# The 16x16 diagonal blocks of the delta rule's triangular inverse: from TensorE to VectorE

## The chip, the core and the metric

The kernel runs on one core of a Trainium2 chip. The metric is the time of one execution in microseconds (us) on the device; lower is better. TensorE (PE in the profile, with PEld for its weight loads) multiplies matrices, VectorE (DVE) and ScalarE (ACT) work elementwise, GpSimd (POOL) does a little, and SyncE (SP) issues DMAs. ScalarE can issue DMAs too, and then spends its own time on each issue. Every engine works through its own list of instructions in order; semaphores hold an instruction back until what it reads is there.

## The reference

Two blocks follow each other: the first with stick-breaking attention, retention and two MLPs, the second with a hybrid mixer and a layer of 16384 experts. There are 256 tokens and a width of 1024. The change touches only the mixer's gated delta rule, which with its 8 heads, after a convolution, reads in short:

```python
G = jnp.cumsum(g, axis=-1)
gamma = jnp.where(incl, jnp.exp(jnp.where(incl, diff, 0.0)), 0.0)      # diff = G_c - G_s
k_beta = k * beta[..., None]
a_mat = jnp.where(strict, jnp.einsum('bnhcd,bnhsd->bnhcs', k_beta, k) * gamma, 0.0) + jnp.eye(CHUNK)
rhs = jnp.concatenate([v * beta[..., None], k_beta * jnp.exp(G)[..., None]], axis=-1)
sol = lax.linalg.triangular_solve(a_mat, rhs, left_side=True, lower=True, unit_diagonal=True)
u, w = sol[..., :DV], sol[..., DV:]
def step(S, inp):                                                       # along the chunks
    v_new = u_c - jnp.einsum('bhcd,bhde->bhce', w_c, S)
    o = jnp.einsum('bhcd,bhde->bhce', qd, S) + jnp.einsum('bhcs,bhse->bhce', at, v_new)
    S = S * dec[..., None, None] + jnp.einsum('bhcd,bhce->bhde', kt, v_new)
```

The matrix `a_mat` is triangular with ones on its diagonal. The kernel inverts it instead of solving with it, in chunks of 128 tokens, and treats the 16 meta tokens that stand ahead of the sequence as a chunk of their own.

## The kernel before

All large matmuls have both factors split into a high and a low part, so a projection is three matmuls for each 128 rows of the contraction (`mm3`, lines 88, 89 and 91). The weights stream through class `Weights`: SyncE loads a `raw` part of 128x1024 (line 247), ScalarE rounds it to `whi` (line 277), VectorE forms the rest, `wlo` (line 278). Four raw and three split parts are in flight. The normalised input, split the same way, comes from `normed`, just ahead of `small_gates`.

`Hybrid.mixers` works the mixer in two halves, q = 0 and 1, each with two units u = 2q and 2q + 1; a unit is two heads, thus four 128x128 blocks (two heads by two chunks). In a half, `main` is the row of projections (names in it: `pq`, `pv`, `pz` for the delta rule, `pqb`, `pvb` for the forgetting attention, `pg` for the gates). Beside it run several generators: the two delta units in lockstep, `meta_state`, the forgetting attention and, in the first half, another stream. `drive` takes a step of each in turn at every `yield`, and a scheduler places what they issue on the engines. So the number of `yield`s decides how many projection matmuls stand between two steps of the delta rule.

`delta_unit` builds `b`, the strictly triangular part of four blocks (tile `bu`, from the product `pkk`), and calls `inverse`, which returns `m`. Later it uses `m` for `pw` and `pvn`. `meta_state` does the same for the meta tokens: one 64x64 matrix that holds four heads' 16x16 blocks (`bm`); its `m` goes into `pvm`, from which the start state `pS0` follows, which both units need. `inverse` doubles the block size at each level l: it transposes `m` (`pt`), multiplies by `b` (`py`, masked to `y`) and by `m` again (`pm`), and subtracts:

```python
nc.vector.scalar_tensor_tensor(m, b, -1.0, mask(0), op0=OP.mult, op1=OP.mult)
...
for l in range(1, levels):
    if l >= 5:
        yield from self.merge(n, e, b, m, t, y, 1 << l)
        continue
    pt = each("pt", lambda o, i: nc.tensor.transpose(o, m[:, i, :], idn))
```

Ahead of the loop `m` is right for blocks of 2. Levels 1, 2 and 3 bring it to 16, level 4 to 32, and `merge` at levels 5 and 6 to 128. The meta matrix has `levels=4` and needs 1 to 3 alone, since its blocks are of 16.

Of the kernel before, what the change touches and what calls it, by code (L numbers as in the profile page):

```python
# [548 lines left out]
class Hybrid:  # L549
# [95 lines left out]
    def small_gates(self):  # L645
# [44 lines left out]
        z = self.ap.tile([128, 2, W], F32, name="cout")  # L690
        nc.vector.memset(z, 0.0)
        self.rows = self.hp.tile([128, W], F32R, name="rows")
        nc.vector.tensor_copy(self.rows, z[:, 0, :])
# [133 lines left out]

    def inverse(self, n, e, b, levels, w):


        k, nc = self.k, self.k.nc
        idn = k.ident[0:e, 0:e]
        shape = [e, n, e]

        def mask(l):
            return self.cmask[0:e, l:l + 1, 0:e].to_broadcast(shape)

        def each(name, f):
            p = self.bank(name)[0:e, 0:n, 0:e]
            for i in range(n):  # L840
                f(p[:, i, :], i)
            return p

        m = w.tile(shape, F32, name=f"m{n}")
        nc.vector.scalar_tensor_tensor(m, b, -1.0, mask(0), op0=OP.mult, op1=OP.mult)
        nc.vector.tensor_tensor(m, m, idn[:, None, :].to_broadcast(shape), op=OP.add)
        yield
        t = w.tile(shape, F32, name=f"t{n}")
        y = w.tile(shape, F32, name=f"y{n}")
        for l in range(1, levels):  # L850
            if l >= 5:
                yield from self.merge(n, e, b, m, t, y, 1 << l)
                continue
            pt = each("pt", lambda o, i: nc.tensor.transpose(o, m[:, i, :], idn))
            nc.scalar.activation(t, pt, AF.Copy)
            yield
            py = each("py", lambda o, i: nc.tensor.matmul(o, b[:, i, :], t[:, i, :], start=True, stop=True))
            nc.vector.tensor_tensor(y, py, mask(l), op=OP.mult)
            yield
            pm = each("pm", lambda o, i: nc.tensor.matmul(o, y[:, i, :], m[:, i, :], start=True, stop=True))  # L860
            nc.vector.tensor_tensor(m, m, pm, op=OP.subtract)
            yield
        return m
# [26 lines left out]

    def meta_state(self, q):

# [5 lines left out]
        nc.tensor.transpose(pt[0:64, 0, :], km, k.ident)  # L898
        nc.tensor.transpose(pt[0:64, 1, :], vm, k.ident)
        sq = w.tile([64, 128], F32, name="msq")  # L900
# [4 lines left out]
        nc.scalar.activation(kt, pt[0:64, 0, :], AF.Copy, scale=ss)  # L905
        v = w.tile([64, 128], F32, name="mv")
        nc.scalar.activation(v, pt[0:64, 1, :], AF.Copy)
        yield
# [30 lines left out]
        nc.vector.scalar_tensor_tensor(b[:, 0, :], pk, col[:, 0:1], gt, op0=OP.mult, op1=OP.mult)  # L939
        m = yield from self.inverse(1, 64, b, 4, w)  # L940
        pv = self.bank("pvm")[0:64, 0, :]
# [14 lines left out]
    def delta_unit(self, u, w):  # L956
# [37 lines left out]
        yield  # L994
        m = yield from self.inverse(4, 128, b, 7, w)
        while u not in self.unit:
# [155 lines left out]
    def mixers(self):  # L1152
        k, nc, a = self.k, self.k.nc, self.k.a
        xn = (klist(k.nh), klist(k.nl))
        with ExitStack() as ctx:
# [14 lines left out]
            self.tile("vm", [128, 8, M])  # L1170

            cum = self.tile("cum", [128, 128 + W])
            nc.vector.memset(cum, 1.0)
# [93 lines left out]
            def meta(q, u):  # L1267
                while u not in rows_v:
                    yield
                yield from self.meta_state(q)  # L1270

# [11 lines left out]
            for q in range(2):  # L1283
# [3 lines left out]
                             main_vb(v), main_z(v), main_qb(v), *([main_gates(3, 6)] if q else []))  # L1287
                drive(main, (delta(q), 1 + q), meta(q, v), forget((1, 2, 3) if q else (0,)),
                      *([] if q else [self.stream()]))
# [530 lines left out]
```

## Time and profile before

| | us |
|---|---|
| median of three runs | 1937.61 |
| fastest and slowest of them | 1937.57, 1942.92 |
| the profiled execution | 1950.35 |
| its span, first to last instruction | 1948.6 |

The profile is of one execution. Its clock of TensorE, as granted, is 0.997 of full speed on average. By engine, TensorE is busy for 99% of the span, VectorE for 73%, ScalarE for 57% and GpSimd for 6%. The mixer lies between about 700 and 1040 us, its halves between 700 and 1020. Weights come in all through the kernel, 332.28 MB are read and 18.87 MB are written.

In rows of instructions, `x4` is a count of instructions taken together; an arrow leads from what is read to what is written (out<-in); the sizes are partitions by elements. `<-DVE wlo L278` behind an idle time says which instruction ended it.

### The profile page before, as it was taken

What the parts mean: (1) busy time and instruction counts of PE and PEld (TensorE: products, weight loads), DVE (VectorE), ACT (ScalarE), POOL (GpSimd) and SP (SyncE); (2) the same over time, 40 slices, a digit from 0 to 9 for tenths busy, and PEclk for the clock granted to TensorE, in tenths of its full rate; (3) what the DMA queues carried; (4) which work ended last, traced back from release to release, by engine and by line L of the source; (5) the groups of instructions that cost most, each with busy time, mean ns of one, the idle gap of its engine ahead of it and who ended that gap; (6) DMA issues with size and microseconds to landing.
All of it is one profiled execution on the core that took longest, in us unless ns stands there. A gap on an engine that the chain in (4) does not pass through costs nothing.

```text
span 1948.6 us, 38035 instructions
## 1 busy us (share of the span) xinstructions
PE 1925.9 (99%) x14787; PEld 1827.2 (94%) x14787; DVE 1427.0 (73%) x2840; ACT 1119.7 (57%) x1761; POOL 116.8 (6%) x187
## 2 busy tenths in 40 slices
PE   8999999999999999999999999999999999999999
PEld 7999999999999989999899999999999998888887
DVE  6575556777655588778676699999888867777776
ACT  7776544655665465545455565446666655555554
POOL 2110000000000100110100111110000000000000
PEclk9999999999999999999899999999999999999999
DMA  6456665555666543222256446776555567777775
GB/s 196 141 164 187 190 186 195 160 179 180 204 186 191 187 158 109 95 90 87 77 173 214 138 163 220 230 227 201 179 177 176 179 198 241 241 240 238 240 239 184
DMA packets 109413, 353.63 MB, mean 181 GB/s; under 512 B 12832, under 2 KB 15664, under 8 KB 109104
## 3 DMA queue, kind: packets, MB, share of 16 engines
q1 hardware_dynamic: 97104, 329.82, 53.8%
q10 hardware_dynamic: 12128, 21.38, 3.4%
q8 instruction: 116, 1.90, 0.4%
q14 instruction: 65, 0.53, 0.1%
HBM read 332.28 MB, written 18.87 MB: 180 GB/s over the span
## 4 chain that ended last, share of the span: by engine, by line
PE 91%; DVE 5%; issue 3%; ACT 1%; DMA 0%; POOL 0%; SPq 0%; DVEq 0%; POOLq 0%; ACTq 0%
PE acc L1597 6%; PE acc L1599 6%; PE acc L1596 6%; PE ph L91 6%; PE ph L88 5%; PE ph L89 5%; PE pd L88 3%; PE pd L91 3%; PE pd L89 3%; PE pu L89 3%; PE pu L91 3%; PE pu L88 3%; PE pg L1565 3%; DVE wlo L278 2%; PE pq L88 2%
## 5 line engine op out<-in xcount | busy, mean ns | idle before, releaser
L278 DVE TENSOR_TENSOR wlo<-raw,whi 128x512 fp32r<-128x512 f32 (+1 forms) x863 | 774.3, 901 | 340.4 <-ACT whi L277 295.2
L277 ACT ACTIVATE whi<-raw 128x512 fp32r<-128x512 f32 (+1 forms) x863 | 674.0, 788 | 603.4 <-PE acc L1597 73.0
L88 PE MATMUL ph<-nh,whi 128*128 128x256 f32 x1024 | 256.1, 285 | 0.4 <-ACT whi L277 0.4
L89 PE MATMUL ph<-nl,whi 128*128 128x256 f32 x1024 | 250.6, 280 | 0.0
L1597 PE MATMUL acc<-whi,cl 128*128 128x512 f32 x504 | 198.1, 393 | 0.0
L1596 PE MATMUL acc<-whi,ch 128*128 128x512 f32 x504 | 196.7, 390 | 0.0
L88 PEld LDWEIGHTS ph<-nh,whi 128*128 128x128 f32 x1024 | 193.3, 189 | 0.6 <-ACT whi L277 0.6
L89 PEld LDWEIGHTS ph<-nl,whi 128*128 128x128 f32 x1024 | 193.4, 189 | 0.0
L91 PE MATMUL ph<-nh,wlo 128*128 128x256 f32 x1024 | 163.2, 282 | 2.1 <-DVE wlo L278 2.0
L1599 PE MATMUL acc<-wlo,ch 128*128 128x512 f32 x504 | 156.2, 391 | 0.0
L91 PEld LDWEIGHTS ph<-nh,wlo 128*128 128x128 f32 x1024 | 138.3, 189 | 3.9 <-DVE wlo L278 3.5
L88 PE MATMUL pu<-nh,whi 128*128 128x256 f32 x512 | 126.7, 282 | 0.0
L89 PE MATMUL pu<-nl,whi 128*128 128x256 f32 x512 | 126.6, 281 | 0.1
L88 PE MATMUL pd<-uh,whi 128*128 128x256 f32 x512 | 123.6, 281 | 0.0
L89 PE MATMUL pd<-ul,whi 128*128 128x256 f32 x512 | 123.5, 281 | 0.0
L1596 PEld LDWEIGHTS acc<-whi,ch 128*128 128x128 f32 x504 | 94.6, 188 | 21.6
L1597 PEld LDWEIGHTS acc<-whi,cl 128*128 128x128 f32 x504 | 94.7, 188 | 20.4
L1599 PEld LDWEIGHTS acc<-wlo,ch 128*128 128x128 f32 x504 | 94.7, 188 | 20.0
L89 PEld LDWEIGHTS pu<-nl,whi 128*128 128x128 f32 x512 | 97.1, 190 | 0.4 <-DVE nl L183 0.3
L89 PEld LDWEIGHTS pd<-ul,whi 128*128 128x128 f32 x512 | 96.9, 189 | 0.0
L88 PEld LDWEIGHTS pu<-nh,whi 128*128 128x128 f32 x512 | 96.7, 189 | 0.1
L88 PEld LDWEIGHTS pd<-uh,whi 128*128 128x128 f32 x512 | 96.7, 189 | 0.0
(553 smaller groups left out, 4226.7 us busy)
## 6 DMA issues: line engine op xcount, KB each, us to landing
raw<-expert_u SPq DMA_DIRECT2D x128, 512.0 KB, 3.8
raw<-expert_v SPq DMA_DIRECT2D x128, 512.0 KB, 4.3
raw<-w_hyb SPq DMA_DIRECT2D x72, 512.0 KB, 3.5
raw<-w_mlp_up SPq DMA_DIRECT2D x64, 512.0 KB, 4.3
raw<-w_mlp_down SPq DMA_DIRECT2D x64, 512.0 KB, 3.6
raw<-w_ret_in SPq DMA_DIRECT2D x48, 512.0 KB, 3.7
spill<-act SPq DMA_DIRECT2D x62, 256.0 KB, 2.8
act<-spill ACTq DMA_DIRECT2D x62, 256.0 KB, 3.7
```

The source lines that it names most:

```text
L88: mm(out, wh[k], xh[k], start=first and k == 0, stop=False, skip_group_check=True)
L89: mm(out, wh[k], xl[k], start=False, stop=False, skip_group_check=True)
L91: mm(out, wl[k], xh[k], start=False, stop=last and k == n - 1, skip_group_check=True)
L277: nc.scalar.activation(hi, src, AF.Copy)
L278: self.last = nc.vector.tensor_tensor(lo, src, hi.bitcast(F32), op=OP.subtract).ins
L1565: nc.tensor.matmul(pg[:, i, :], A[:, i, :], B[:, i, :], start=True, stop=True)
L1596: mm(acc[t][d], c0[i][t], vh, start=False, stop=False, skip_group_check=True)
L1597: mm(acc[t][d], c1[i][t], vh, start=False, stop=False, skip_group_check=True)
L1599: mm(acc[t][d], c0[i][t], vl, start=False, stop=False, skip_group_check=True)
```

## The change

Levels 1 to 3 leave `inverse`; its loop begins at 4. In their place the 16x16 diagonal blocks of a half, 32 for each unit and 4 for the meta matrix, are laid one on each of 68 partitions and inverted there by VectorE. To get there, ScalarE writes `b` to a DRAM tile `bd` (`to_solve`, one DMA for each of three matrices), and SyncE loads the diagonal blocks of it into `bs` (nine DMAs). `solve` works from the last row of the inverse upward: 15 times a product over the rows below (`bt`) and a sum of it into one row of `bx`. ScalarE then writes the blocks with nine DMAs into DRAM tiles `zd` and `zm` that hold zeros elsewhere; six DMAs in `small_gates` write these zeros, each from a zero tile. SyncE loads `zd` and `zm` as `m`. `bx` and `bs` are one buffer each for both halves. `meta_state` now begins when the keys' rows are there (`rows_k`), no longer the values', and takes up its values behind the writing of `b`. Both kinds of matrix wait in the program's text until `solve` has issued its writes (`self.solved`).

```diff
--- before.py
+++ after.py
@@ -689,6 +689,10 @@
 
         z = self.ap.tile([128, 2, W], F32, name="cout")
         nc.vector.memset(z, 0.0)
+        for t in self.zd:
+            nc.scalar.dma_start(t, z.rearrange("p a t -> p (a t)")[:, 0:512].rearrange("p (i t) -> p i t", i=4))
+        for t in self.zm:
+            nc.scalar.dma_start(t, z[0:64, 0:1, 0:64])
         self.rows = self.hp.tile([128, W], F32R, name="rows")
         nc.vector.tensor_copy(self.rows, z[:, 0, :])
         k.split(self.rows[0:8], self.rows[32:40], pc)
@@ -825,7 +829,51 @@
         nc.scalar.activation(eb, pg, AF.Exp)
         return pg, gt, eb
 
-    def inverse(self, n, e, b, levels, w):
+    def blocks(self, t, e, n):
+
+        return bass.AP(t.tensor, t.offset, [[e, n], [16 * n * e + 16, e // 16], [n * e, 16], [1, 16]])
+
+    def to_solve(self, q, part, b, e, n):
+
+        nc = self.k.nc
+        yield
+        t = self.dram.tile([e, n, e], F32, name=f"bd{q}{part}")
+        nc.scalar.dma_start(t, b)
+        x = self.bs[q][part:part + n * e // 16]
+        for i in range(n):
+            nc.sync.dma_start(x[i * e // 16:(i + 1) * e // 16], self.blocks(t, e, n)[i])
+        self.given[q] += 1
+        yield
+
+    def solve(self, q):
+
+
+        nc = self.k.nc
+        while self.given[q] < 3:
+            yield
+        for _ in range(3):
+            yield
+        b = self.bs[q]
+        x = self.hp.tile([68, 16, 16], F32, name="bx")
+        tmp = self.hp.tile([68, 225], F32, name="bt")
+        nc.vector.tensor_copy(x, self.eye)
+        for s in range(14, -1, -1):
+            n = 15 - s
+            t = tmp[:, 0:n * n].rearrange("p (c t) -> p c t", c=n)
+            nc.vector.scalar_tensor_tensor(t, x[:, s + 1:16, s + 1:16].rearrange("p t c -> p c t"), -1.0,
+                                           b[:, s:s + 1, s + 1:16].to_broadcast([68, n, n]), op0=OP.mult, op1=OP.mult)
+            nc.vector.tensor_reduce(x[:, s, s + 1:16], t, axis=AX.X, op=OP.add)
+            if s in (9, 4):
+                yield
+        yield
+        for part, e, n, t in ((0, 128, 4, self.zd[2 * q]), (32, 128, 4, self.zd[2 * q + 1]), (64, 64, 1, self.zm[q])):
+            for i in range(n):
+                nc.scalar.dma_start(self.blocks(t, e, n)[i], x[part + i * e // 16:part + (i + 1) * e // 16])
+        self.solved.add(q)
+        yield
+
+    def inverse(self, n, e, b, z, levels, w):
+
 
 
         k, nc = self.k, self.k.nc
@@ -842,12 +890,14 @@
             return p
 
         m = w.tile(shape, F32, name=f"m{n}")
-        nc.vector.scalar_tensor_tensor(m, b, -1.0, mask(0), op0=OP.mult, op1=OP.mult)
-        nc.vector.tensor_tensor(m, m, idn[:, None, :].to_broadcast(shape), op=OP.add)
-        yield
+        nc.sync.dma_start(m, z)
+        for _ in range(3):
+            yield
+        if levels < 5:
+            return m
         t = w.tile(shape, F32, name=f"t{n}")
         y = w.tile(shape, F32, name=f"y{n}")
-        for l in range(1, levels):
+        for l in range(4, levels):
             if l >= 5:
                 yield from self.merge(n, e, b, m, t, y, 1 << l)
                 continue
@@ -888,7 +938,7 @@
             nc.scalar.activation(m[p, :, q], pm[p, 0:n, q], AF.Copy)
         yield
 
-    def meta_state(self, q):
+    def meta_state(self, q, values):
 
         k, nc, w = self.k, self.k.nc, self.mp
         km, vm = (x[:, 4 * q:4 * q + 4, :] for x in (self.km, self.vm))
@@ -896,15 +946,12 @@
         cum, bones = self.cmask[0:64, 8, 0:64], self.cmask[0:64, 9, 0:64]
         pt = self.bank("ptk")
         nc.tensor.transpose(pt[0:64, 0, :], km, k.ident)
-        nc.tensor.transpose(pt[0:64, 1, :], vm, k.ident)
         sq = w.tile([64, 128], F32, name="msq")
         ss = w.tile([64, 1], F32, name="mss")
         nc.scalar.activation(sq, pt[0:64, 0, :], AF.Square, accum_out=ss)
         self.rsqrt(ss, ss, 1.0)
         kt = w.tile([64, 128], F32, name="mkt")
         nc.scalar.activation(kt, pt[0:64, 0, :], AF.Copy, scale=ss)
-        v = w.tile([64, 128], F32, name="mv")
-        nc.scalar.activation(v, pt[0:64, 1, :], AF.Copy)
         yield
         pb = self.bank("pbk")
         nc.tensor.transpose(pb[:, 0, 0:64], kt, k.ident[0:64, 0:64])
@@ -937,7 +984,17 @@
         nc.tensor.matmul(pk, kf, kf, start=True, stop=True)
         b = w.tile([64, 1, 64], F32, name="bm")
         nc.vector.scalar_tensor_tensor(b[:, 0, :], pk, col[:, 0:1], gt, op0=OP.mult, op1=OP.mult)
-        m = yield from self.inverse(1, 64, b, 4, w)
+        yield from self.to_solve(q, 64, b, 64, 1)
+        while not values():
+            yield
+        pt = self.bank("ptv")
+        nc.tensor.transpose(pt[0:64, 0, :], vm, k.ident)
+        v = w.tile([64, 128], F32, name="mv")
+        nc.scalar.activation(v, pt[0:64, 0, :], AF.Copy)
+        yield
+        while q not in self.solved:
+            yield
+        m = yield from self.inverse(1, 64, b, self.zm[q], 4, w)
         pv = self.bank("pvm")[0:64, 0, :]
         nc.tensor.matmul(pv, m[:, 0, :], v, start=True, stop=True)
         vn = w.tile([64, 128], F32, name="vnm")
@@ -992,7 +1049,10 @@
         nc.gpsimd.affine_select(gt, gt, pattern=[[0, 4], [1, 128]], compare_op=OP.is_ge, fill=0.0, base=0,
                                 channel_multiplier=-1)
         yield
-        m = yield from self.inverse(4, 128, b, 7, w)
+        yield from self.to_solve(u // 2, 32 * (u % 2), b, 128, 4)
+        while u // 2 not in self.solved:
+            yield
+        m = yield from self.inverse(4, 128, b, self.zd[u], 7, w)
         while u not in self.unit:
             yield
         v, qf, rq = self.unit[u]
@@ -1169,6 +1229,16 @@
             self.tile("km", [128, 8, M])
             self.tile("vm", [128, 8, M])
 
+
+            self.dram = pool("solve", 1, space=bass.MemoryType.DRAM)
+            self.bs = [self.hp.tile([68, 16, 16], F32, name="bs")] * 2
+            self.given, self.solved = [0, 0], set()
+            self.zd = [self.dram.tile([128, 4, 128], F32, name=f"zd{u}") for u in range(4)]
+            self.zm = [self.dram.tile([64, 1, 64], F32, name=f"zm{q}") for q in range(2)]
+            self.tile("eye", [68, 16, 16])
+            nc.vector.memset(self.eye, 1.0)
+            nc.gpsimd.affine_select(self.eye, self.eye, pattern=[[1, 16], [-1, 16]], compare_op=OP.is_equal, fill=0.0,
+                                    base=0, channel_multiplier=0)
             cum = self.tile("cum", [128, 128 + W])
             nc.vector.memset(cum, 1.0)
             nc.vector.tensor_copy(cum[:, 0:128], self.cmask[:, 7, :])
@@ -1265,9 +1335,9 @@
                     forgotten.add(u)
 
             def meta(q, u):
-                while u not in rows_v:
+                while u not in self.rows_k:
                     yield
-                yield from self.meta_state(q)
+                yield from self.meta_state(q, lambda: u in rows_v)
 
             def chain(*gens):
                 for g in gens:
@@ -1285,7 +1355,7 @@
                 main = chain(main_k(u), main_k(v), main_kb(u), main_v(u), main_kb(v), main_v(v),
                              self.key_norms(q, self.fb), main_vb(u), main_q(u), main_qb(u), main_q(v), main_z(u),
                              main_vb(v), main_z(v), main_qb(v), *([main_gates(3, 6)] if q else []))
-                drive(main, (delta(q), 1 + q), meta(q, v), forget((1, 2, 3) if q else (0,)),
+                drive(main, (delta(q), 1 + q), meta(q, v), self.solve(q), forget((1, 2, 3) if q else (0,)),
                       *([] if q else [self.stream()]))
 
     def gate(self, gt, p, r=None):
```

Lines behind the first hunk carry higher numbers in the changed kernel: `pt`, `py` and `pm` at 854, 857 and 860 become 904, 907 and 910.

The first place is SyncE's queue in the first half of the mixer. `raw` are the weights (`w_hyb` the mixer's, `peer_wq` the expert layer's), `gspill` a store of gate values, `bd_...` the three DRAM copies of `b`, `zd_8124` and `zd_8125` the solved blocks of the first half's two units:

```order
-L247 DMA raw<-w_hyb 128x1024 x53
-L247 DMA raw<-peer_wq 128x1024 x3
+L1324 DMA gspill<-cout 256x1x256
+L247 DMA raw<-w_hyb 128x1024 x9
+L844 DMA bs<-bd_8881 8x16x16 x4
+L247 DMA raw<-w_hyb 128x1024 x4
+L844 DMA bs<-bd_8979 8x16x16 x2
+L844 DMA bs<-bd_8937 4x16x16
+L844 DMA bs<-bd_8979 8x16x16 x2
+L247 DMA raw<-w_hyb 128x1024 x8
+L893 DMA m_9159<-zd_8124 128x512
+L893 DMA m_9166<-zd_8125 128x512
```

Before, only weights stand here. Now nine loads of diagonal blocks (4, 2, 1 and 2) lie between them, and behind eight further weights the loads of `m`, which wait for the writes of the solved blocks; that of the meta matrix and 17 weight loads stand behind the two shown.

The second place is TensorE's row where a delta unit's inverse begins. Before, this is the first level of unit 0, right behind its `pkk`; `pv` is the projection of the values, `ptv` a transpose of them:

```order
L986 MATMUL pkk<-kf 128x128 x4
L854 MATMUL pt<-ident,m_8742 128x128 x4
L91 MATMUL pv<-nh,wlo 128x272 x3
L807 MATMUL ptv<-ident,cout 128x128 x4
L91 MATMUL pv<-nh,wlo 128x272
L88 MATMUL pv<-nh,whi 128x272
L89 MATMUL pv<-nl,whi 128x272
L88 MATMUL pv<-nh,whi 128x272
L857 MATMUL py<-t_8821,bu 128x128 x4
```

In the changed kernel the first instructions that read an `m` stand further down, among the projection `pvb`: `pvm` reads the meta matrix's, `pt` those of units 0 and 1:

```order
L999 MATMUL pvm<-mv,m_9161 64x128
L88 MATMUL pvb<-nh,whi 128x272
L89 MATMUL pvb<-nl,whi 128x272
L88 MATMUL pvb<-nh,whi 128x272
L89 MATMUL pvb<-nl,whi 128x272
L1008 MATMUL pS_9259<-vnm,kth 128x128 x4
L1302 MATMUL ptv<-ident,cout 128x128 x4
L1306 MATMUL ptvm<-ident,cout 16x128 x2
L904 MATMUL pt<-ident,m_9159 128x128 x4
L904 MATMUL pt<-ident,m_9166 128x128 x4
L777 MATMUL ptq<-ident,qf 128x128 x4
L907 MATMUL py<-t_9309,bu 128x128 x4
```

The level that was first is gone; the one that is now first is level 4, the meta matrix's `pvm` comes ahead of it, and the two units' transposes stand side by side, with few matmuls between `pvm` and them.

The third place is VectorE's list at the start of the first half's `solve` (`bt` the products, `bx` the rows of the inverse). `cin` belongs to the norm of the keys, `rows` to the forgetting attention:

```order
L863 SCALAR_TENSOR_TENSOR bt<-bx,bs 68x1
L770 SCALAR_TENSOR_TENSOR cin<-cin 4x272
L865 TENSOR_REDUCE bx<-bt 68x1
L768 TENSOR_TENSOR cin<-cin 4x272
L863 SCALAR_TENSOR_TENSOR bt<-bx,bs 68x4
L769 SCALAR_TENSOR_TENSOR cin<-cin 4x272
L865 TENSOR_REDUCE bx<-bt 68x2
L770 SCALAR_TENSOR_TENSOR cin<-cin 4x272
L863 SCALAR_TENSOR_TENSOR bt<-bx,bs 68x9
L278 TENSOR_TENSOR wlo<-raw,whi 128x1024
L865 TENSOR_REDUCE bx<-bt 68x3
L1141 TENSOR_TENSOR rows<-cin 4x272
```

The solve's instructions have others between them, weight splits `wlo` among them.

## Rows read from the trace of the kernel before

**Rows 1.** The page, its first part:

```profile
span 1948.6 us, 38035 instructions
...
PE 1925.9 (99%) x14787; PEld 1827.2 (94%) x14787; DVE 1427.0 (73%) x2840; ACT 1119.7 (57%) x1761; POOL 116.8 (6%) x187
```

**Rows 2.** Windows: us, busy (count) of PE, PEld, DVE, ACT, POOL; TensorE clock; DMA:

```profile
700.00:740.00 40.00, 39.60 (x300) 36.00 (x299) 37.54 (x99) 27.66 (x53) 1.54 (x7) 1.00 0.47 153
...
sum 320.00, PE 317.23 PEld 293.03 DVE 252.73 ACT 173.07 POOL 25.22; mean PE 39.65 PEld 36.63 DVE 31.59 ACT 21.63 POOL 3.15
```

**Rows 3.** The list of TensorE's waits, 700 to 1040: total us, times, longest:

```profile
PE pto L1058 <- DVE on L1054: 0.8, 2, 0.6
```

**Rows 4.** Timeline of TensorE, 752.4 to 755.5: start, us, instruction:

```profile
752.45 0.66 PE L854 MATMUL pt<-ident,m 128*128 128x128 f32 x4
752.95 1.06 PE L860 MATMUL pm<-m,y 128*128 128x128 f32 x8
753.76 0.37 PE L91 MATMUL pv<-nh,wlo 128*128 128x272 f32 x1
754.08 1.16 PE L857 MATMUL py<-t,bu 128*128 128x128 f32 x8
755.00 0.50 PE L91 MATMUL pv<-nh,wlo 128*128 128x272 f32 x2
```

**Rows 5.** Timeline of TensorE, 939.0 to 939.3:

```profile
939.02 0.33 PE L860 MATMUL pm<-m,y 64*64 64x64 f32 x2
939.27 0.39 PE L88 MATMUL pq<-nh,whi 128*128 128x260 f32 x1
```

**Rows 6.** Groups of VectorE, 700 to 1000: busy us, mean ns, idle before:

```profile
L858 DVE TENSOR_TENSOR y<-py,cmask 128x512 f32<-128x512 f32 x16 | 11.0, 688 | 4.3 <-PE py L857 4.3
```

**Rows 7.** Timeline of VectorE, 755.9 to 758:

```profile
755.89 1.22 DVE L278 TENSOR_TENSOR wlo<-raw,whi 128x1024 fp32r<-128x1024 f32 x1
757.02 0.50 DVE L742 SCALAR_TENSOR_TENSOR cout<-cin,conv,cout 128x272 f32<-128x272 f32 x1
757.43 0.15 DVE L917 TENSOR_TENSOR bgs<-pst,hsel 64x8 f32<-64x8 f32 x1
757.55 0.50 DVE L742 SCALAR_TENSOR_TENSOR cout<-cin,conv,cout 128x272 f32<-128x272 f32 x1
```

**Rows 8.** The instruction of line 672: ns, start:

```profile
L672 ACTq DMA_DIRECT2D al<-a_log x1: 334/334/334, 684.0 to 684.0; - x1
```

**Rows 9.** DMA issues: count, KB each, us from issue to landing:

```profile
spill<-act SPq DMA_DIRECT2D x62, 256.0 KB, 2.8
act<-spill ACTq DMA_DIRECT2D x62, 256.0 KB, 3.7
...
cmask<-cmask ACTq DMA_DIRECT2D x1, 640.0 KB, 6.2
...
vec<-vec ACTq DMA_DIRECT2D x1, 1.5 KB, 2.5
...
al<-a_log ACTq DMA_DIRECT2D x1, 4.0 KB, 3.2
```

**Rows 10.** Timeline of TensorE, 953.5 to 957.5:

```profile
953.58 0.28 PE L88 MATMUL pqb<-nh,whi 128*128 128x256 f32 x1
...
955.00 0.28 PE L88 MATMUL pqb<-nh,whi 128*128 128x256 f32 x1
```

**Rows 11.** Timeline of TensorE, 926 to 928.5:

```profile
926.64 0.29 PE L88 MATMUL pvb<-nh,whi 128*128 128x272 f32 x1
...
928.14 0.28 PE L88 MATMUL pvb<-nh,whi 128*128 128x272 f32 x1
```

**Rows 12.** Window of 941 to 951, columns as in rows 2:

```profile
941.00:951.00 10.00, 10.00 (x52) 8.85 (x51) 3.60 (x7) 4.37 (x10) 2.60 (x2) 0.51 0.16 50
```

**Rows 13.** Timeline of TensorE, 947.2 to 947.5:

```profile
947.20 0.42 PE L88 MATMUL pq<-nh,whi 128*128 128x260 f32 x1
947.41 0.42 PE L89 MATMUL pq<-nl,whi 128*128 128x260 f32 x1
```

## The prediction

> **What bounds the kernel now.** I began with the page's first two parts: TensorE is busy for 1925.9 of 1948.6 us [rows 1]. Busy is not yet bound, so I went on to the windows of the stretch in which the change lies, the two halves of the hybrid mixer, 700 to 1020 us: TensorE 317.23 of 320 us, VectorE 252.73, ScalarE 173.07, and in the first 40 us VectorE is at 37.54 [rows 2]. The list of TensorE's waits decides it: the longest total from 700 to 1040 us is 0.8 us [rows 3]. TensorE stands in one program order, and every instruction finds its data there when its turn comes. So a matmul taken out is worth its step (the time to the next start), and a wait put into that row is paid in full.
>
> **What goes from TensorE.** In `inverse`, levels 1 to 3 of a delta unit go, each with four transposes `pt`, four products `py` and four `pm`; a float32 product shows as two records. The steps of one such level in a dense place: the transposes 0.50 us (752.45 to 752.95), `pm` 0.81, `py` 0.92 [rows 4], 2.23 us together. Four units by three levels: 26.8 us. A meta block's level is one transpose and two products of 64x64; `pm` takes 0.25 us (939.02 to 939.27) [rows 5], `py` has the same size, for the transpose I take 0.15: 0.65 us, six times, 3.9 us. In all 30.7 us. With the smaller step for both products and 0.4 for the transposes it is 27, with the larger for both 32. Nothing lies beside these matmuls on TensorE, so this is gained wherever the engine has other work in its row; the projections are that work.
>
> **VectorE and ScalarE.** VectorE loses eight instructions of 128x512 for each unit at about 0.69 us (`y` on line 858 [rows 6], `m` on 861 of the same size, and the two that made the first `m`): 22 us. It gains two solves. Of their sizes the trace has none; the nearest rows are a step of 0.41 us for 272 elements and 0.12 us for 8 [rows 7], so 0.11 us and 1.1 ns an element. A solve has 15 products and 15 sums over 1, 4, ... 225 elements, 1240 for each kind: 30 x 0.11 + 2480 x 0.0011 = 6.0 us; with dependent pairs back to back somewhat more, I take 6.5, at most 8. The sum for VectorE is a relief of 9 us, which is worth nothing by itself. ScalarE loses twelve copies and gains 30 DMA starts of 0.33 us [rows 8], 10 us; about even, and it has room.
>
> **What the change adds: four DMAs in a chain.** For each pair of units now stands, before level 4: blocks to DRAM (ScalarE), blocks back to 68 partitions (SyncE), solve (VectorE), nine writes of the solved blocks (ScalarE), three loads of `m` (SyncE). I count it from the meta block's product `pkk`, since the solve needs all three block sets and that one is last.
>
> First half, from that `pkk`: VectorE has four `bu`, three small ones and two 272-element ones before it ends `bm`, +3.2 us. A short DMA: 128 runs of 32 bytes landed 3.2 us after issue (`al`), 128 runs of 12 bytes in 2.5 (`vec`) [rows 9]; I take 3.2, so DRAM has the block at +6.5. SyncE then issues it and two more at 0.33 us each, the last lands at +10.7. VectorE itself comes to the solve at +10.0, so it waits under 1 us. Between the solve's instructions the order puts five weight splits `wlo` (step 1.13 us [rows 7]), fourteen instructions of some 270 elements and a few more: 12.8 us. With 6.5 the solve ends at +30. The nine writes take 9 x 0.33 us to start, and the eighth has to wait until the second has landed, since they share a completion lane: the last starts 3.9 us later and lands 3.2 after that. Then the loads: `m` of 256 KB like `act<-spill`, 3.7 us [rows 9]. All are there 10.7 us after the solve, at +40.7.
>
> TensorE's row from `pkk` to the first instruction that needs an `m` (`pvm`, line 999): 44 matmuls of a `pvb`, 48 of `pq`, 48 of `pqb`, 48 of `pq`, 48 of `pz`, 28 of `pvb`, and some 18 short ones. Twelve matmuls of 256 columns take 1.42 us [rows 10], twelve of 272 take 1.50 [rows 11]: 5.5 + 5.8 + 5.7 + 5.8 + 5.7 + 3.5 + 2.3 = 34.3 us. So TensorE comes at +34.3, finds nothing until +40.7 and stands 6.4 us.
>
> Second half, the same way: `bm` at +1.2, the blocks back at +8.2 (one DMA behind it, not three), 20 us of solve with six `wlo` between, +28.2; here TensorE needs only the first unit's `m` at once: four writes and a load, 4.5 + 3.9 = 8.4, +36.6. TensorE's row up to `pt` (line 904): 41 + 48 + 48 + 48 + 48 matmuls and short ones, 30.1 us. It stands 6.5 us.
>
> Together 12.9 us. If every DMA lands like `vec`, each chain is 3.3 us shorter and 6 us remain; if each needs the 6.2 us of `cmask` [rows 9], each is 11.5 us longer, 36 us. I take 12.9, because `al`, `spill` and `act` lie at 2.8 to 3.7 and are nearest in size.
>
> Before I took that value I weighed a rule that speaks against it. In the trace, short runs cost a read nothing: `al` with runs of 32 bytes lands in 3.2 us, 256 KB of `spill` in 2.8 [rows 9]. The Trainium skill (DMA: Bandwidth & Descriptors, Specifications) says that below 512 bytes a DMA engine does a read-modify-write; the eighteen write-backs go out in runs of 64 bytes. No row here shows a short write to DRAM, so the rule is neither borne out nor refuted; what slow transfers would do is the third rival below.
>
> **The rest.** The zeros: six DMA starts on ScalarE among the splits of the normalised input (`normed`), for which TensorE waits at that place: 6 x 0.33 us = 2.0 us if none is hidden, 0 if all; I take 1.0. What is queued behind the waits: on SyncE the weight loads behind `m` stand until the write-backs land, 7 us; six loads are ahead of TensorE (four raw, three split; one is used in 2.9 us), some 17 us, so that is covered. On ScalarE the weight split behind the nine writes comes 4.5 us late and TensorE stops for it, but inside the 6.4 us already counted. VectorE's copy of `eye` for the second half waits for the same write-backs, about 1 us, with nothing urgent behind it. After both halves the gates' projections still stand behind the delta rule's last matmul, so a late unit isn't exposed at the end. Moving the transpose of `vm` is free.
>
> **Sum.** -30.7 + 12.9 + 1.0 = -16.8 us in the profiled execution, 1950.35 us (span 1948.6 and 1.75 around it): 1933.5. The three timed runs have a median of 1937.61, 0.65% less; scaled, the gain is 16.7 and the time 1920.9 us.
>
> **Rivals.**
> 1. The chain is covered. For it: the order was laid out so that TensorE has filler, and every other wait in this stretch fits to within 0.8 us [rows 3]. Against: four landings in a row, each of which my rows put at 2.5 us or more. Gain 30.7 - 1 = 29.7, 1908 us.
> 2. The stops cost clock. The trace has one stretch, 941 to 951 us, with a granted clock of 0.51, the lower level (1.2 of 2.4 GHz) [rows 12]; small products of 64x64 as in [rows 5] stand just before it, and matmuls of 260 columns start 0.21 us apart there [rows 13], where those of 256 and 272 otherwise take 0.12 [rows 10, 11]. Such a fall costs 10 us x 0.49 = 4.9 us. If both stops bring one, the gain is 16.8 - 9.8 = 7.0, 1930.7 us. For it: these stops are longer than any TensorE has now. Against: the one fall seen had no idle time before it, and might itself go. The Trainium skill (TensorE: Matmul & The Clock Gate, HAM oscillation) describes just this, a wait for a DMA after which the next matmuls run cold; no stop of that length is in this trace to test it.
> 3. The other side, slower: the write-backs and block loads are slow, because hundreds of 64-byte runs go to and from DRAM between weight loads. Place: `pvm` and `pt`. At 6.2 us a landing the stops are 36 us, +6 in all, with two falls of the clock +16, 1953 us. It decides from about 5.4 us a landing, where the stops eat the 29.7. For it: `cmask` at 6.2 and no row of a short write. Against: the four other kinds (`spill`, `act`, `vec`, `al`), 2.5 to 3.7 [rows 9].
> 4. Between them, landings near 5 us: no change, 1932 to 1943 us.
>
> **Chances.** Forecast 0.50, rival 1 0.17, rival 2 0.13, rival 4 0.10, rival 3 0.10. The forecast's own range is 1912 to 1930 (landings of 2.5 to 4.2 us, one fall more or none). The range for 8 in 10 goes from 1906, just under rival 1, to 1938, which takes in rival 2 and half of rival 4. What can be told from no change is 0.3%, 5.8 us; rival 2 lies near that bound, and I give 0.04 of it to no change: faster 0.76, the same 0.14, slower 0.10.
>
> **What would show it.** Right: 24 products `py` of 128x128 fewer in each half; two stops of TensorE, at `pvm` in the first half and at `pt` in the second, of about 6 us, released by a DMA; solves of 6 to 8 us busy; short DMAs landing in 2.5 to 3.7 us; the mixer some 17 us shorter and nothing else changed. Wrong: stops under 2 us or over 12, a second or third stretch at half clock, VectorE late with `wlo` so that TensorE waits for it, or a weight load that comes late behind `m`.

## The result and the profile after

The changed kernel takes 1914.53 us (median of 4 runs, 1911.93 to 1921.52) against 1937.59; the ratio is 0.9886, interval 0.9849 to 0.9923, so 22 us less (15 to 29). A second set of runs beside other kernels gave 0.9904 (0.9873 to 0.9935), 18.6 us less. The forecast was 16.7 us. One execution of the kernel with the split write-backs (4206 us) and one of that with three queues and the zeros (3773 us) were far slower, the cause unknown, and are left out of the ratios below.

The page's first part, which answers to [rows 1]:

```profile
span 1912.9 us, 37569 instructions
...
PE 1882.5 (98%) x14517; PEld 1784.4 (93%) x14517; DVE 1413.9 (74%) x2855; ACT 1110.4 (58%) x1743; POOL 119.3 (6%) x188
```

The spans differ by 35.7 us, more than the medians. 8.1 us of that lie ahead of the mixer, where both run the same code, and 6.3 behind it (more below). So I compare one stretch of every trace, from the first `pbaf` (in `small_gates`) to the first `ph` (in the expert layer). Its windows, columns as in [rows 2], first before, then after:

```profile
702.60:1163.80 461.20, 458.43 (x3789) 433.51 (x3788) 360.42 (x935) 252.39 (x484) 38.23 (x69) 0.99 0.39 128
```

```profile
694.50:1134.40 439.90, 429.47 (x3519) 405.99 (x3518) 347.93 (x948) 244.66 (x467) 38.84 (x69) 0.99 0.44 143
```

21.3 us less: TensorE has 270 records fewer and 29.0 us less busy time, but 10.4 us idle in place of 2.8. The end of this stretch, behind the mixer's last `pp`, has the same 1155 matmul records in these two and in all traces below but that of each solve twice, and takes 134.1 to 136.9 us from trace to trace. The mixer alone, up to that `pp`, is therefore the steadier measure. Before and after (a second trace of the changed kernel, below, has 303.4):

```profile
702.60:1029.40 326.80, 324.03 (x2634) 299.71 (x2633) 257.85 (x714) 177.08 (x353) 26.59 (x54) 0.98 0.34 110
```

```profile
694.50:998.00 303.50, 293.07 (x2364) 270.15 (x2363) 244.92 (x727) 169.26 (x335) 27.18 (x54) 0.98 0.40 129
```

The list of TensorE's waits, 680 to 1040 us, answers to [rows 3]:

```profile
PE pvb L88 <- ACT whi L277: 2.9, 2, 2.4
PE pt L904 <- DMA m<-zd: 1.5, 1, 1.5
PE pvb L91 <- DVE wlo L278: 1.0, 1, 1.0
PE pto L1118 <- DVE on L1114: 0.9, 2, 0.5
PE pks L1152 <- DVE rows L1141: 0.8, 1, 0.8
PE pbaf L651 <- DVE nl L151: 0.8, 2, 0.5
```

The first stop is not at `pvm`. TensorE's timeline around it:

```profile
781.45 0.66 PE L91 MATMUL pvb<-nh,wlo 128*128 128x272 f32 x4
784.49 0.39 PE L88 MATMUL pvb<-nh,whi 128*128 128x272 f32 x1 [2.38 <-ACT whi L277]
...
786.71 1.27 PE L91 MATMUL pvb<-nh,wlo 128*128 128x272 f32 x4 [0.96 <-DVE wlo L278]
...
788.83 0.69 PE L999 MATMUL pvm<-mv,m 64*64 64x128 f32 x2
```

ScalarE's timeline says why: it issues the nine write-backs in one piece, 5.4 us long, and the weight split comes after them. With the microsecond for which it waits for the solve ahead of them it does no other work for 6.5 us (the 6.49 in the row of `cin`).

```profile
777.37 4.78 ACTq L871 DMA_DIRECT2D zd<-bx  x8
782.49 0.25 ACTq L871 DMA_DIRECT2D zm<-bx  x1
782.86 0.63 ACT L748 ACTIVATE cin<-cout 128x512 f32<-128x512 f32 x1 [6.49 <-DMA zd<-bx]
783.39 1.04 ACT L277 ACTIVATE whi<-raw 128x1024 fp32r<-128x1024 f32 x1
```

When `pvm` comes, its `m` has landed. But TensorE's clock is at the lower level by then (windows, the last three numbers are its clock, the DMA share and GB/s):

```profile
784.00:788.00 4.00, 2.56 (x13) 2.34 (x14) 3.74 (x4) 1.86 (x3) 1.33 (x2) 0.74 0.46 142
788.00:792.00 4.00, 4.00 (x16) 3.17 (x16) 0.59 (x2) 1.82 (x3) 0.00 (x0) 0.50 0.77 246
792.00:796.00 4.00, 4.00 (x20) 3.62 (x19) 0.00 (x0) 2.12 (x5) 0.00 (x0) 0.50 0.02 6
796.00:800.00 4.00, 4.00 (x36) 3.94 (x35) 2.65 (x8) 1.13 (x2) 0.00 (x0) 0.98 0.00 0
```

From 784 to 800 us that is 4 x (0.26 + 0.50 + 0.50 + 0.02) = 5.1 us of full-speed time. The stretch at half clock of [rows 12] isn't in this trace. In the second half the stop is where it was forecast, at the first unit's `pt`, and short; SyncE issued the load of that `m` at 924.32 us. The three timelines, TensorE's, SyncE's and ScalarE's:

```profile
926.96 0.66 PE L904 MATMUL pt<-ident,m 128*128 128x128 f32 x4 [1.46 <-DMA m<-zd]
```

```profile
894.86 0.24 SPq L844 DMA_DIRECT2D bs<-bd  x1
898.54 21.68 SPq L247 DMA_DIRECT2D raw<-w_hyb  x7
924.32 1.15 SPq L893 DMA_DIRECT2D m<-zd  x2
```

```profile
892.94 0.47 ACTq L841 DMA_DIRECT2D bd<-bm  x1
...
920.20 3.63 ACTq L871 DMA_DIRECT2D zd<-bx  x8
923.87 0.33 ACTq L871 DMA_DIRECT2D zm<-bx  x1
```

The solves, VectorE's products and sums (busy us, mean ns, idle before):

```profile
L863 DVE SCALAR_TENSOR_TENSOR bt<-bx,bs 68x1 f32<-68x1 f32 (+14 forms) x30 | 9.1, 305 | 0.2
L865 DVE TENSOR_REDUCE bx<-bt 68x1 f32<-68x1 f32 (+14 forms) x30 | 6.9, 230 | 0.2
```

### The profile page after: what moved, and what is told of

It reads as the page before. It is cut to its first block, busy times and chain, and to the rows that moved or that the text cites. A ratio compares the mean times of both kernels' runs of the same rounds, so it can differ in the third digit from the quotient of the medians.

```text
span 1912.9 us, 37569 instructions
## 1 busy us (share of the span) xinstructions
PE 1882.5 (98%) x14517; PEld 1784.4 (93%) x14517; DVE 1413.9 (74%) x2855; ACT 1110.4 (58%) x1743; POOL 119.3 (6%) x188
## 4 chain that ended last, share of the span: by engine, by line
PE 87%; DVE 9%; issue 1%; ACT 1%; DMA 1%; POOL 0%; ACTq 0%; DVEq 0%; SPq 0%; POOLq 0%
PE acc L1669 6%; PE acc L1666 6%; PE acc L1667 6%; PE ph L91 5%; PE ph L88 5%; PE ph L89 5%; DVE wlo L278 3%; PE pd L88 3%; PE pd L91 3%; PE pd L89 3%; PE pu L89 3%; PE pu L91 3%; PE pu L88 3%; PE pg L1635 3%; PE pv L88 2%; PE pv L89 2%
## 5 line engine op out<-in xcount | busy, mean ns | idle before, releaser
L88 PE MATMUL ph<-nh,whi 128*128 128x256 f32 x1024 | 251.5, 282 | 0.0
L89 PE MATMUL ph<-nl,whi 128*128 128x256 f32 x1024 | 245.5, 277 | 0.0
```

The source lines that it names most:

```text
L88: mm(out, wh[k], xh[k], start=first and k == 0, stop=False, skip_group_check=True)
L89: mm(out, wh[k], xl[k], start=False, stop=False, skip_group_check=True)
```

## The experiments

Theory A: the removed matmuls are gained in full; what is lost again is lost where ScalarE's held list stops TensorE, and in the clock behind that stop. The rivals: VectorE's new load, or solved blocks that come late whoever writes them.

**Without the chain.** In `inverse`, with `to_solve`, `solve` and the zeros emptied:

```diff
-        nc.sync.dma_start(m, z)
+        nc.vector.scalar_tensor_tensor(m, b, -1.0, mask(0), op0=OP.mult, op1=OP.mult)
+        nc.vector.tensor_tensor(m, m, idn[:, None, :].to_broadcast(shape), op=OP.add)
```

> Levels 1 to 3 are left out as in the changed kernel, and so is all that replaces them: no write of the blocks, no solve, no write-back, no zeros; `m` is formed by the two VectorE instructions of before and is right for blocks of 2 alone, so the delta rule's result is not the reference's. The `yield`s stay. It prices the removed matmuls by themselves. Theory A (the freed TensorE time is used in full, what the changed kernel loses again lies in its two stops): 30.7 us of matmuls and the 4.9 us of the half-clock stretch at 941 us go, a gain of 31 to 36 us on the kernel before, 1902 to 1907 us, and 9 to 13 us under the changed kernel. Rival B (the projections cannot use the freed time, since weight splits or loads limit them then): about the changed kernel's 1914 us, with TensorE waiting for `whi` or `wlo`.

Measured: 0.9822 (0.9797 to 0.9848), 34.5 us (29 to 39) under the kernel before; in the stretch 35.9 us less, no half clock; the stretch, then the mixer alone:

```profile
694.80:1120.10 425.30, 420.75 (x3519) 399.89 (x3518) 341.64 (x899) 243.29 (x466) 38.84 (x69) 1.00 0.42 139
```

```profile
694.80:985.00 290.20, 285.64 (x2364) 265.39 (x2363) 239.11 (x678) 167.99 (x335) 27.21 (x54) 1.00 0.38 124
```

Theory A gave 31 to 36; in the traces it would be 35.6, the 4.9 us of [rows 12] among them. So the chain costs the changed kernel 439.9 - 425.3 = 14.6 us in the stretch, and 303.5 - 290.2 = 13.3 us in the mixer alone.

**The kernel before without the meta block's levels.**

```diff
-        m = yield from self.inverse(1, 64, b, 4, w)
+        m = yield from self.inverse(1, 64, b, 1, w)
```

> The kernel before, with the meta block's levels 1 to 3 left out (its `m` is right for blocks of 2 alone, so the start state is not the reference's); all else stays. Theory A (the half-clock stretch of before at 941 to 951 us hangs on the meta block's 64x64 products that stand just before it): 3.9 us of matmuls and 4.9 us of half clock go, some 9 us, 1928 to 1930 us, and no window of 20 us in the mixer under 0.9 of the clock. Rival B (the stretch hangs on something else, so its going in the changed kernel is chance or another effect): the stretch stays, 3 to 5 us, 1933 to 1935 us.

Measured: 0.9967 (0.9947 to 0.9987), 6.4 us; in the stretch 453.7, so 7.5 us, and the clock stays up:

```profile
940.00:960.00 20.00, 19.86 (x166) 19.30 (x164) 15.84 (x52) 9.10 (x17) 2.04 (x3) 1.00 0.36 125
```

This agrees with theory A, but doesn't show it. Each timed execution has its mean granted clock on record. A fall that costs 4.9 of 1937 us leaves 0.997 at most; of the forty timed executions of the kernel before, beside these experiments, 31 are at 0.999 or 1.000. So most of them have no such stretch, with the 64x64 products in place, and one trace without it can't tell whether it went with them. By time, the interval (2.5 to 10.3 us) holds the 3.9 us of matmuls alone. The order moved too: the second half's `pvm` stands 94 projection matmuls earlier.

**The write-backs by SyncE, and by ScalarE and SyncE.**

```diff
-                nc.scalar.dma_start(self.blocks(t, e, n)[i], x[
+                nc.sync.dma_start(self.blocks(t, e, n)[i], x[                             # the first
+                (nc.sync if part else nc.scalar).dma_start(self.blocks(t, e, n)[i], x[    # the second
```

> The eighteen write-backs are issued by SyncE in place of ScalarE. Theory A (in the first half TensorE stops because the weight split stands behind nine writes in ScalarE's list, and the clock falls after that stop): the stop of 2.4 and 1.0 us at `pvb` is gone, the clock stays at 1.00 from 780 to 800 us, 6 to 9 us less than the changed kernel, 1906 to 1909 us. Rival B (the solved blocks themselves come too late, whichever queue writes them): the stop moves to `pvm` or `pt` and the time stays within 3 us of 1914.5. Rival C (SyncE's weight loads, now behind the solve, come late): TensorE or ScalarE waits for `raw`, over 1917 us.

> The write-backs of a half's first unit stay on ScalarE (four), those of the second unit and of the meta block go to SyncE (five). Theory A: ScalarE is held for 1.3 us in place of 5, so the stop at `pvb` is under 1 us and the clock stays up; 5 to 9 us less than the changed kernel, 1906 to 1910 us. Rival B (late data): a stop at `pvm` or `pt` of the same 3 us and the clock falls all the same, within 3 us of 1914.5.

Measured: 0.9892 (0.987 to 0.9914) and 0.9864 (0.9834 to 0.9895). By time neither can be told from the changed kernel, so the gain forecast is not shown. In the stretch they take 433.9 and 432.9 us, 4 to 7 less than the changed kernel's two traces (439.9 and 438.2). With SyncE alone the clock stays up, but the order of instructions differs too (`pvm` stands 35 matmuls later) and a new stop takes the place of the old:

```profile
PE pvb L88 <- DVE z L1278: 1.9, 1, 1.9
```

With the split the stop of 2.4 us is gone, that of 1.0 us for `wlo` stays, and a shorter fall is left, 0.91 from 780 to 800 us:

```profile
780.00:800.00 20.00, 18.70 (x133) 17.30 (x132) 12.15 (x18) 10.05 (x18) 1.33 (x2) 0.91 0.59 188
```

**The changed kernel again.**

> The changed kernel itself, once more, so that the kernels beside it are compared on one chip. From its first runs and the spread seen since: 0.9865 to 0.9905 of the kernel before. Theory A (the half-clock stretch after the first half's stop is brought by that stop, a property of this order of instructions): a window under 0.8 of the clock at 780 to 800 us again. Rival D (whether a stop brings it is chance): the stop is there and the clock stays up.

Measured: 0.9904 (0.9873 to 0.9935), the stretch 438.2 us, and stop and fall as before:

```profile
PE pvb L88 <- ACT whi L277: 2.8, 2, 2.3
...
PE pvb L91 <- DVE wlo L278: 1.0, 1, 1.0
```

```profile
780.00:800.00 20.00, 16.78 (x99) 15.07 (x98) 8.85 (x18) 8.67 (x15) 1.33 (x2) 0.74 0.31 87
```

The fall came behind this stop in both traces. The mean clocks say how often: of the changed kernel's ten timed executions eight are at 0.996 or 0.997, which leaves room for a fall of 5.1 us; one at 0.998 and one at 0.999 have none. Of the ten executions of the two kernels with three queues below, none is under 0.999. So the stop brings the fall mostly, but not always.

**Each solve twice.**

```diff
-        nc.vector.tensor_copy(x, self.eye)
-        for s in range(14, -1, -1):
+        for s in [*range(14, -1, -1)] * 2:
+            if s == 14:
+                nc.vector.tensor_copy(x, self.eye)
```

> Each solve is done twice on VectorE, the second time from a fresh copy of `eye`; 7 to 8 us more VectorE work in each half, between the blocks' arrival and the write-backs. In the instruction order of TensorE the first `pvm` then stands about 105 matmuls later, the second 134, which is 12 to 16 us of projections. Theory A (the chain from `pkk` to `m` is covered by projections as far as the order puts them in between; only what the order leaves uncovered is paid): 0 to 4 us over the changed kernel, stops of the same size, 1914 to 1919 us. Rival B (the chain is on the path and each us of it is paid, as the prediction reckoned): 13 to 16 us more, 1928 to 1931 us.

Measured: 0.9931 (0.9907 to 0.9955), 5 us over the changed kernel beside it; the stretch 448.2, 8 to 10 over. It lies between the two forecasts: of 16 us more of VectorE work a third is paid by time, about half in the stretch. The order moved further than the text has it, by 134 and 171 projection matmuls at `pvm`. What is paid isn't where rival B has it: the longest wait is that of the meta block's transpose in the second half, ahead of that half's chain, for a norm that VectorE comes to late, and behind it the clock falls several times:

```profile
PE pbk L958 <- DVE cin L770: 3.3, 1, 3.3
```

```profile
880.00:960.00 80.00, 71.99 (x521) 67.14 (x521) 59.46 (x158) 37.44 (x65) 6.75 (x6) 0.91 0.44 140
```

80 us at 0.91 are 7.2 us. But the changed kernel's fall of 5.1 us in the first half isn't there, so the clock's part in the difference is some 2 us. The larger part is idle time of TensorE, 17.0 us in place of 10.2 (the stretch, this kernel and then the changed kernel beside it):

```profile
693.50:1141.70 448.20, 431.21 (x3520) 406.66 (x3518) 364.30 (x1010) 244.85 (x467) 41.39 (x69) 0.98 0.44 140
```

```profile
693.10:1131.30 438.20, 427.96 (x3519) 404.30 (x3518) 347.61 (x946) 243.94 (x467) 38.72 (x69) 0.99 0.44 143
```

**Three queues; the split with the zeros by SyncE; three queues and the zeros.**

```diff
-                nc.scalar.dma_start(self.blocks(t, e, n)[i], x[
+                (nc.scalar, nc.gpsimd, nc.sync)[part // 32].dma_start(self.blocks(t, e, n)[i], x[
...
-            nc.scalar.dma_start(t, z[0:64, 0:1, 0:64])
+            nc.sync.dma_start(t, z[0:64, 0:1, 0:64])
```

> The write-backs of a half are issued by three engines: the first unit's by ScalarE (four), the second's by GpSimd (four), the meta block's by SyncE (one). Theory A (ScalarE's held list made the first stop): ScalarE is held 1.3 to 3 us, no stop over 1 us at a `pvb`, 4 to 7 us less than the changed kernel, 1907 to 1911 us. Rival B (late data): within 2 us of it. Rival C (GpSimd's DMAs start or land late): a stop at the second unit's `pt`, over 1916 us.

> As the kernel with the write-backs split between ScalarE and SyncE, and the six DMAs that write the zeros are issued by SyncE too. Theory A (the zeros on ScalarE delay the splits of the normalised input): the waits at `pbaf` go from 0.8 to 0.2 us, 1 us less than with the zeros on ScalarE, 5 to 8 us less than the changed kernel, 1906 to 1910 us. Rival (the zeros, behind weight loads on SyncE or ahead of them, delay a `raw`): TensorE waits for `whi` near 700 us and the gain is gone.

> The write-backs are issued by three engines (the first unit's by ScalarE, the second's by GpSimd, the meta block's by SyncE) and the zeros by SyncE. Theory A (two separate costs, ScalarE's held list and the zeros among the splits): the waits at `pbaf` go as they did with the zeros on SyncE alone, the stops at `pvm` and `pt` stay at 1.0 to 1.3 us, no stretch at half clock in the mixer, 428 to 430 us from the first `pbaf` to the first `ph`, and 0.983 to 0.986 of the kernel before. Rival (the two repairs overlap, or the earlier `pvm` waits longer): 431 us or more there, and 0.986 to 0.989.

Measured: 0.985 (0.9821 to 0.9879), 0.9852 (0.9823 to 0.9881), 0.9855 (0.9824 to 0.9887); the stretches 430.2, 429.8 and 428.4 us. They can't be told from each other by time; in the stretch they are 8 to 12 us under the changed kernel, whose two ratios are 0.3 to 0.5% higher, with intervals that overlap: by time alone the gain over the changed kernel is not shown. The third of them in the stretch, and the two waits that are left at the `m`s:

```profile
694.20:1122.60 428.40, 422.21 (x3520) 400.01 (x3519) 349.59 (x948) 244.12 (x467) 44.34 (x77) 1.00 0.45 147
```

```profile
PE pt L904 <- DMA m<-zd: 1.0, 1, 1.0
PE pvm L999 <- DMA m<-zm: 1.0, 1, 1.0
```

With the weight splits no longer held the blocks do come last, but only by a microsecond. Where SyncE writes the zeros, `pbaf` waits 0.3 us in place of 1.3 and 1.1, and the stretch is shorter than with the zeros on ScalarE by 1.8 us (430.2 to 428.4) and 3.1 us (432.9 to 429.8, of which 1.8 is clock). The mixer alone of the third kernel takes 294.0 us. So of the 13.3 us that the chain costs there, 9.5 go with the queues that issue its DMAs, the clock behind the stop among them, and 3.8 stay (one trace each, and the order differs a little: the first `pvm` stands 17 matmuls earlier).

**The solves beside.** As without the chain, with both solves on VectorE and in `to_solve` only

```diff
+        nc.vector.tensor_copy(self.bs[q][0:64, 14, 15:16], b[0:64, 0, 0:1])
```

> As the kernel without the chain (levels 1 to 3 left out, `m` right for blocks of 2 alone, no DMAs of blocks or zeros), but VectorE does both solves in their place, on a tile of zeros that takes one column from each `b` so that a solve cannot begin before the three are there; nothing reads what it solves. It parts the chain's cost into VectorE's load and the rest. Theory A (the solves cost TensorE little, only the waits at `pks` behind the keys' norm, 1.3 us, and the rest is DMA, ScalarE's list and clock): 426 to 428 us from the first `pbaf` to the first `ph` (425.3 without the solves), 0.982 to 0.984 of the kernel before. Rival B (VectorE's 15 us of solves are what the 14 us of the chain are paid for): 433 us or more there, 0.986 or more.

Measured: 0.9841 (0.9814 to 0.9868) and 426.3 us in the stretch, 1.0 over the kernel without solves:

```profile
695.10:1121.40 426.30, 421.41 (x3520) 399.22 (x3518) 351.37 (x964) 243.00 (x467) 41.19 (x69) 1.00 0.43 139
```

Rival B falls by the stretch, though the ratio is at the upper edge of theory A's: VectorE's load is 1 us of the 14.6 in the stretch, and 2.0 of the 13.3 in the mixer alone (292.2 less 290.2).

## Why the prediction came out right, step by step

- **The matmuls taken out, 30.7 us.** Right: without the chain the stretch is 35.9 us shorter, 30.7 and the 4.9 of [rows 12]; by time it is 34.5 (29 to 39). Of the two bounds beside it the lower comes to 28.1 by its own steps (12 x 2.02 + 3.9), not 27.
- **The half clock of before.** The sum is made for the profiled execution and gives nothing to this stretch, though rival 2 says that the fall "might itself go". In the traces it went; without it the 21.3 and 23.0 us of the stretch would be 16.4 and 18.1. For the timed runs nothing was nearly right, because most executions of the kernel before have no such stretch. The prediction had no such reason, so this was luck.
- **TensorE's own row, 34.3 and 30.1 us.** This was mis-sized, and it is the main reason why the second stop came out at 1.5 us in place of 6.5. From the meta block's `pkk` TensorE reaches `pt` after 34.1 us, not 30.1: 32.8 us of work, and 1.3 us of waits at `pks` that the count doesn't have (0.8 in the list above, 0.5 below). In the first half it was at +35.4 when the split stopped it, with 16 matmuls still ahead of `pvm`.

```profile
891.38 0.33 PE L984 MATMUL pkk<-mkf 128*64 128x64 f32 x2
```

```profile
891.38:925.50 34.12, 32.81 (x255) 30.27 (x254) 28.40 (x74) 17.53 (x32) 2.93 (x4) 1.00 0.42 130
```

```profile
PE pks L1152 <- DVE fk L1154: 0.5, 1, 0.5
```

- **The chain up to the `m`s, +40.7 and +36.6.** Nearly right. In the second half the solve ends at +28.8 (forecast +28.2), and `m` is there at +35.6. So of the 5.0 us by which that stop was put too long, 4.0 are TensorE's row and 1.0 the chain. In the first half the meta matrix's load went out at +37.4 and `pvm` found it landed at +42.1.
- **The chain and the zeros, 12.9 + 1.0.** 14.6 and 12.9 us measured (the changed kernel twice, less 425.3), but made otherwise: against the kernel without the chain 5.9 us more idle time (10.4 less 4.5) and 5.1 us of half clock; of the remaining 3.6, 1.3 lie behind the mixer, where nothing differs, and the rest I can't place. Two stops of 6.4 and 6.5 us came to 3.3 and 2.0 (1.5 at `pt` and 0.5 for a `whi` behind it). That the total nearly agrees is luck: the stops are less than half as long, and the fall of the clock isn't in the sum.
- **Where the first stop lies.** The text has the weight split behind nine writes, "inside the 6.4 us already counted". It was the stop, and the `m`s were there behind it. ScalarE's held time was mis-sized: the last write starts 5.1 us after the first, not 3.9 (3.7 in the second half). One of the first half's issues alone took 1.8 us, where the others took 0.3 to 0.5; why, the trace doesn't show:

```profile
L871 ACTq DMA_DIRECT2D zd<-bx x16: 271/344/1775, 777.4 to 923.6; - x16
```

- **Landings.** Somewhat too long in the sum. The short block went out at 892.94 us and SyncE loaded it back from 894.86, at most 1.9 us in place of 3.2; the 256 KB `m` took at most 926.96 - 924.32 = 2.6 in place of 3.7. The first unit's four write-backs of 64-byte runs start from 920.20 on, and the load that waits for them starts at 924.32, after 4.1 us, where the sum has 4.5. The Trainium skill (DMA: Bandwidth & Descriptors, Specifications) has a read-modify-write below 512 bytes; no price of it shows here, since writes as slow as the third rival's would have made this longer than forecast.
- **The solve, 6.5 us.** 8.0 (9.1 + 6.9 for two), the upper end. It cost TensorE 1.0 to 2.0 us, by the solves beside.
- **Rival 2, two falls.** One came, of 5.1 us, behind the longer stop; behind the stop of 1.5 us none did. The Trainium skill (TensorE: Matmul & The Clock Gate, HAM oscillation) has a wait followed by cold matmuls; both traces of the changed kernel agree for that first stop, the waiting being for a split held behind DMAs.
- **Rivals 1, 3 and 4** did not occur. Rival 1 is nearly what the kernel with three queues and the zeros moved does: 3.1 us over the one without the chain.
- **Its signs.** Two of the signs of being wrong came: a stop under 2 us, at `pt`, and TensorE waiting for a late `wlo`, 1.0 us.

## What to carry to other kernels

Where an engine issues DMAs and also feeds the bound engine, count what stands behind the issues in its list: nine in one piece held ScalarE for 5.4 us, and TensorE stood 3.3 us for the splits behind them, more than VectorE's whole new load cost it. Spread write-backs over the queues that have least behind them. In a forecast of a stop, count the bound engine's own row as carefully as the chain that it waits for: here the row was 4 us off and the chain 1. And before a stretch at half clock goes into a sum, look at the mean clock of the other executions: one trace may have it and most executions not.

## What the runs showed that I had not expected

The same stop brings a fall of the clock in one execution and not in another. In the expert layer TensorE waits 2.3 us for `sc` in each trace (the row is that of the changed kernel's list of waits). In the changed kernel's first trace the clock stays up behind it, in the second it falls, as it does in seven of the twelve traces:

```profile
PE pt L1602 <- DVE sc L1599: 2.3, 1, 2.3
```

```profile
1300.00:1320.00 20.00, 17.27 (x148) 16.70 (x147) 19.56 (x54) 13.72 (x22) 1.47 (x2) 1.00 0.66 213
```

```profile
1300.00:1320.00 20.00, 17.43 (x135) 16.96 (x133) 18.55 (x50) 13.93 (x22) 1.47 (x2) 0.91 0.61 187
```

And the same matmul has two durations, each kept over a long stretch. The first MLP's from 200 us on (minimum, median, maximum in ns), before and after:

```profile
L88 PE MATMUL pu<-nh,whi x46: 281/281/282, 199.8 to 215.6; 128*128 128x256 f32 x46
```

```profile
L88 PE MATMUL pu<-nh,whi x36: 276/276/276, 200.1 to 211.6; 128*128 128x256 f32 x36
```

That is 1.8% there; in the second MLP both traces have 281. When the mixer begins they are 8 us apart, with the granted clock at 1.00 in both. Such differences are why two single executions can't be compared by their spans here, and they go into the 0.3% that 5 runs leave open. Which of the two a stage gets, nothing here explains.
